# Expert pairs fed by an indirect DMA of stored rows, with the overflow branch behind the output

## The chip, the core and the metric

The kernel runs on one core of a Trainium2 chip. TensorE (PE) multiplies, VectorE (DVE) and ScalarE (ACT) work elementwise, GpSimd (POOL) and SyncE (SP) here mostly issue DMAs. The metric is the device time of one execution in microseconds, the median over the runs of a kernel. Lower is better.

## The reference, cut to what matters

Two transformer layers on 256 tokens of width 1024, all in float32. The second ends in a mixture of 16 experts, which is the part that the change touches:

```python
x = x + gate1 * (merged @ w_out[l])
h2 = rmsnorm(x, norm2_g[l]) * (1.0 + scale2) + shift2
y = hierarchical_moe(h2, ...)         # top-1 group of 4, then top-2 of its 4 experts
x = x + gate2 * y
return rmsnorm(x, final_g)

# in hierarchical_moe
for e in range(N_EXPERTS):            # 16 experts, width 512
    act = jax.nn.silu(hf @ w_gate[e]) * (hf @ w_up[e])
    out = out + combine[:, e:e + 1] * (act @ w_down[e])
```

`combine` is zero for all but two experts of a token, so 256 tokens make 512 uses of an expert.

## The kernel before

The 256 tokens lie in two tiles of 128 rows (`t` = 0, 1) in the slab `X`. All but the experts is matrix work on all tokens; its order was made by a planner with estimated costs (class `Order`). The expert part is written out by hand in `build` (from line 1972) and is not planned: the instructions of an engine stand in the order in which the code calls them.

**The expert pairs.** Two experts at a time are worked on, eight pairs, p = 0 to 7. Each expert takes up to 64 tokens (`CAP`), so a pair fills 128 columns. `routing` gives each token its place `pos` in each expert and its weight `comb`. For each pair:

- `one_hot` (L1493, DVE) compares `pos` with 1 to 64 and makes a 0/1 matrix of tokens by places, and a copy of it multiplied by each token's norm factor `rs`.
- `gather` (L1508) multiplies X by that copy on PE, in sixteen float32 matmuls of 128 columns. The result is the pair's tokens, transposed, in two PSUM banks. ACT empties the first and DVE the second, with the scale and shift of the norm (`ra`).
- `expert_pair` (L1566) runs gate, up and down. One expert works in the left 64 columns of the PE array and one in the right. `w` = 0 is gate, `w` = 1 is up; each has two halves, `q` = 0, 1. Then h = silu(gate) * up on DVE, four transposes of h, ACT's copy `th` of them, and down in two halves of 512 columns.
- `way_back` (L1527) transposes the 0/1 matrix and multiplies it by `comb`; `scatter` (L1547) adds the pair's result to all 256 tokens in four PSUM banks with it.

`mid` is a tuple of functions that `expert_pair` calls on its way: `mid[0]` behind gate (`way_back`), `mid[1]` behind up and ahead of the transposes of h (`gather` of the pair after), `mid[2]` ahead of down (`scatter` of the last half of the pair before), `mid[3]` behind the second half of down.

**Weights.** A pair's weights are twelve chunks of 1 MB, loaded by SP in the order of use, each into a slab from a free list. When the last matmul on a chunk has run, its slab goes back to the list and SP issues the next load into it (`release`, `pump`). Pair 7's last loads, twelve of them, are of 512 KB.

**Overfull experts.** `cnt` is the largest count of an expert. Where it is over 64, `overflow` computes the rest; it is a branch that all engines take or skip, at `mid[3]` of pair 6 (L2007). With these inputs the branch is skipped. The final norm and four output stores follow pair 7.

Of the kernel before, what the change touches and what calls it, by code (L numbers as in the profile page):

```python
# [20 lines left out]
P = 128  # L21
D = 1024
# [24 lines left out]
def constants():  # L47
    i = np.arange(P)
    le = (i[:, None] <= i[None, :]).astype(np.float32)
    lt = (i[:, None] < i[None, :]).astype(np.float32)  # L50
    ge = (i[:, None] >= i[None, :]).astype(np.float32)
    row = i % 64
    head = row % 8
    here = (row < 16) & (head % 2 == i // 64)
    pick = [here & (head // 4 == g) for g in range(2)]
    high = [(row < 8) & (head // 2 % 2 == b) for b in range(2)]
    low = [(row >= 8) & (head // 2 % 2 == b) for b in range(2)]
    fox = np.stack(pick + high + low, axis=1).astype(np.float32)
    fox[:, 2:] *= -1
    cf = np.concatenate(  # L60
        [
            np.eye(P, dtype=np.float32),
            lt,
            np.broadcast_to(np.arange(1, CAP + 1, dtype=np.float32), (P, CAP)),
            np.broadcast_to(np.arange(4, 0, -1, dtype=np.float32), (P, 4)),
            fox,
        ],
        axis=1,
    )
# [251 lines left out]
class Body:  # L321
    def __init__(self, ctx, tc, a, pack):
# [8 lines left out]
        self.big = ctx.enter_context(tc.tile_pool(name="big", bufs=1))  # L331
        self.ps = ctx.enter_context(tc.tile_pool(name="ps", bufs=1, space=bass.MemoryType.PSUM))
# [374 lines left out]
    def setup(self):  # L707
# [4 lines left out]
        self.cf = self.small([P, 2 * P + CAP + 10], "cf")  # L712
# [34 lines left out]
        self.fox = self.cf[:, 2 * P + CAP + 4:]  # L747
# [597 lines left out]
    def res_half(self, t, b, bank):  # L1345
# [13 lines left out]
        if b == 1:  # L1359
            task = self.o.spawn(self.res_scale(t))  # L1360
# [64 lines left out]
    def routing(self):  # L1425
# [60 lines left out]
        self.comb = s("comb", 16)  # L1486
        tt(self.comb.rearrange("p t (g e) -> p t g e", g=4), gb, o1, OP.mult)
# [5 lines left out]
    def one_hot(self, p):  # L1493

        v = self.nc.vector
        buf = self.turn_of("sp").rearrange("p (i t s) -> p i t s", i=2, t=2)
        for t in range(2):
            g, r = buf[:, 0, t], buf[:, 1, t]
            v.tensor_tensor(
                g.rearrange("p (e s) -> p e s", e=2),  # L1500
                self.iota.unsqueeze(1).to_broadcast([P, 2, CAP]),
                self.pos[:, t, 2 * p:2 * p + 2].unsqueeze(2).to_broadcast([P, 2, CAP]),
                OP.is_equal,
            )
            v.tensor_scalar(r, g, self.rs[:, t, 0:1], None, OP.mult)
        return buf

    def gather(self, g):  # L1508

        nc = self.nc  # L1510
        x = self.tmp("ra", 1, D).rearrange("p (k s) -> p k s", k=8)
        for b in range(2):
            ps = self.turn_of("w")
            for j in range(4):
                k = 4 * b + j
                for t in range(2):
                    self.mm(ps[:, j * P:(j + 1) * P], self.x[:, t, k * P:(k + 1) * P], g[:, 1, t], t == 0, t == 1)
            for j in range(4):
                k = 4 * b + j
                out, q = x[:, k], ps[:, j * P:(j + 1) * P]  # L1520
                if b:
                    nc.vector.tensor_scalar(out, q, self.a2[:, k:k + 1], self.modc[:, 3, k:k + 1], OP.mult, OP.add)
                else:
                    self.act(out, q, AF.Identity, scale=self.a2[:, k:k + 1], bias=self.modc[:, 3, k:k + 1])
        return x

    def way_back(self, p, g):  # L1527

        nc = self.nc
        ps = self.turn_of("w")
        for t in range(2):
            self.tr(ps[:, t * P:(t + 1) * P], g[:, 0, t])
        for t in range(2):
            self.mm(ps[:, 256:258], g[:, 0, t], self.comb[:, t, 2 * p:2 * p + 2], t == 0, t == 1)
        gts = []
        for dt in (F32R, F32) if p == 7 else (F32R,):
            gt = self.turn_of("sp")[:, 0:256].bitcast(dt).rearrange("p (t s) -> p t s", t=2)
            self.act(gt, ps[:, 0:256].rearrange("p (t s) -> p t s", t=2), AF.Copy)  # L1540
            gts.append(gt)
        cs = self.tmp("cs", 2, 4)
        for e in range(2):
            nc.vector.tensor_copy(cs[e * 64:(e + 1) * 64, 0:1], ps[e * 64:(e + 1) * 64, 256 + e:257 + e])
        return gts, cs
# [20 lines left out]
    def expert_pair(self, p, x, cs, mid, last=None):  # L1566
# [3 lines left out]
        for w in range(2):  # L1570
            ps = self.turn_of("w")
            for q in range(2):
# [60 lines left out]
    def overflow(self):  # L1633
# [4 lines left out]
        xn = self.sq[0].rearrange("p (t n) -> p t n", t=2)  # L1638
        self.h2 = self.sq[1].rearrange("p (k n) -> p k n", k=8)
        for t in range(2):  # L1640
            self.act(xn[:, t], self.x[:, t], AF.Copy, scale=self.rs[:, t, 0:1])
# [4 lines left out]
        nc.vector.tensor_tensor(co, co, self.comb, OP.mult)  # L1646
# [9 lines left out]
        for e in range(16):  # L1656
# [19 lines left out]
            for t in range(2):  # L1676
                for b in range(2):
# [7 lines left out]
                    y = self.sq[0][:, :512]  # L1685
# [19 lines left out]
    def build(self):  # L1705
# [261 lines left out]
        self.spare(["PP"])  # L1967
# [5 lines left out]
        nxt = self.gather(g)  # L1973
# [4 lines left out]
        for p in range(8):  # L1978
# [10 lines left out]
            def m0(p=p, g=g, prev=prev):  # L1989
# [3 lines left out]
                return self.way_back(p, g)  # L1993

            def m1(ahead=ahead):
                if ahead is not None:
                    box["n"] = self.gather(ahead)
# [16 lines left out]
            prev = self.expert_pair(p, cur, S["pair", p], (m0, m1, m2, m3), self.square if p == 7 else None)  # L2014
# [3 lines left out]
        self.final_norm()  # L2018

    def final_row(self):  # L2020

        self.sums = self.small([P, 2, 3], "sums")
        self.pre = self.small([P, 2], "pre")
        row = self.slab(self.free.pop(), "row_f")
# [23 lines left out]
    def final_norm(self):  # L2048
        nc, v = self.nc, self.nc.vector
        m = self.small([P, 2], "fm")  # L2050
        r = self.small([P, 2], "fr")
        q = self.small([P, 2], "fq")
# [65 lines left out]
```

## Time and profile before

| | us |
|---|---|
| median of 3 runs | 726.47 (726.34 to 728.13) |
| the profiled execution | 727.37 |
| its span in the trace | 725.6 |
| from the first gate matmul of pair 0 to that of pair 7 | 489.0 to 686.7 |

Times in rows are us from the start of the span; a row's second number is how long it lasts. In brackets stands how long the engine idled before, and what ended that. Each float32 matmul has several records in the trace, so that the sixteen matmuls of a gather are 32 records.

### The profile page before, as it was taken

Reading aid. Unit: us, or ns where it says so; the run is one execution under the profiler, and the core shown is the slowest. Engines: PE = TensorE matmul, PEld = TensorE weight load, DVE = VectorE, ACT = ScalarE, POOL = GpSimd, SP = SyncE. Lnnn points to the kernel's source line nnn. Section 1 sums busy time; section 2 is a strip of 40 time slices with the busy share of each in tenths; the row PEclk is TensorE's granted clock in tenths of the full one; section 3 lists DMA queues with packets and bytes.
Section 4 is the critical chain, followed back from the end, with each engine's and each line's share of the span. In section 5 each row is a group of like instructions: output and inputs, shape, how many; then the busy total and the mean of one; then the engine's idle time right before and its main releaser. Section 6 shows DMA issues by size and latency. Waiting matters only on the chain. (4 is left out here: it accounts for less than half of the span.)

```text
span 725.6 us, 10217 instructions
## 1 busy us (share of the span) xinstructions
PE 699.8 (96%) x4028; PEld 506.9 (70%) x4030; DVE 400.4 (55%) x744; ACT 314.6 (43%) x607; POOL 2.2 (0%) x8
## 2 busy tenths in 40 slices
PE   6999999999999988999999999989999999999994
PEld 5999889878878867898877778884344453453432
DVE  6586696896766785768868666452221221212315
ACT  6654465564445586636578545321111110111113
POOL 0000000000000000000000000000000000000000
PEclk9999999999999999999999999989999999999998
DMA  9966666556856661574747957977999999999601
GB/s 359 366 238 229 236 237 231 204 201 217 306 182 228 220 235 63 208 286 163 294 161 280 357 224 293 372 321 322 415 420 423 420 421 421 420 422 416 248 1 58
DMA packets 30373, 201.64 MB, mean 278 GB/s; under 512 B 3825, under 2 KB 4337, under 8 KB 7153
## 3 DMA queue, kind: packets, MB, share of 16 engines
q1 hardware_dynamic: 29968, 200.82, 71.1%
q8 instruction: 33, 0.54, 0.3%
q10 hardware_dynamic: 288, 0.11, 0.1%
q14 instruction: 20, 0.16, 0.1%
q0 software_dynamic: 64, 0.01, 0.0%
HBM read 199.88 MB, written 1.05 MB: 277 GB/s over the span
## 5 line engine op out<-in xcount | busy, mean ns | idle before, releaser
L274 DVE TENSOR_TENSOR w<-ring,w 128x1024 fp32r<-128x1024 f32 (+1 forms) x166 | 156.7, 965 | 80.5 <-ACT w L274 80.1
L274 ACT ACTIVATE w<-ring 128x1024 fp32r<-128x1024 f32 (+1 forms) x166 | 136.3, 849 | 88.8 <-PE d L433 82.0
L433 PE MATMUL d<-w,H 128*128 128x512 f32 x448 | 138.8, 391 | 0.9 <-DVE w L274 0.9
L433 PE MATMUL d<-H,w 128*128 128x256 f32 x672 | 121.8, 283 | 0.0
L433 PEld LDWEIGHTS d<-H,w 128*128 128x128 f32 x672 | 104.6, 192 | 0.1
L433 PE MATMUL d<-w,L 128*128 128x512 f32 x224 | 91.9, 410 | 6.0 <-DVE L L274 6.0
L433 PEld LDWEIGHTS d<-w,H 128*128 128x128 f32 x448 | 84.1, 188 | 18.8 <-DVE w L274 1.6
L433 PE MATMUL d<-L,w 128*128 128x256 f32 x336 | 97.0, 289 | 0.0
L433 PEld LDWEIGHTS d<-L,w 128*128 128x128 f32 x336 | 64.4, 192 | 1.2 <-issue 1.0
L433 PE MATMUL d<-w,YA 128*128 128x512 f32 x224 | 60.6, 394 | 0.0
L433 PEld LDWEIGHTS d<-w,L 128*128 128x128 f32 x224 | 42.1, 188 | 17.0 <-DVE L L274 7.5
L433 PE MATMUL w<-ring,ra 128*64 128x512 f32 x152 | 50.2, 595 | 1.6 <-PEq L2007 1.6
L274 DVE SCALAR_TENSOR_TENSOR acc<-ring,ca,acc 128x1024 f32<-128x1024 f32 x39 | 49.9, 1281 | 1.8 <-DMA ring<-weights 1.6
L433 PEld LDWEIGHTS d<-w,YA 128*128 128x128 f32 x224 | 41.8, 188 | 8.9 <-issue 0.3
L274 ACT ACTIVATE ra<-w,modc,a 128x128 f32<-128x128 f32 x32 | 12.0, 455 | 66.3 <-PE w L433 66.3
L274 ACT ACTIVATE rg<-th 128x512 fp32r<-128x512 f32 x15 | 9.4, 630 | 62.2 <-DVE th L1614 43.6
L274 ACT ACTIVATE th<-w 128x512 f32<-128x512 f32 (+1 forms) x16 | 9.3, 584 | 62.3 <-PE w L433 49.9
L1590 DVE TENSOR_TENSOR th<-th,w 128x512 f32<-128x512 f32 (+1 forms) x9 | 5.6, 628 | 50.2 <-PE w L433 50.2
L433 PEld LDWEIGHTS w<-sp,X 128*128 128x128 f32 x256 | 29.2, 192 | 5.7 <-issue 5.7
L1614 DVE SCALAR_TENSOR_TENSOR th<-w,cs,acc 128x512 f32<-128x512 f32 (+1 forms) x17 | 12.2, 718 | 36.1 <-PE w L433 36.1
L433 PE MATMUL w<-sp,X 128*128 128x128 f32 x256 | 30.7, 278 | 0.0
L433 PEld LDWEIGHTS w<-ring,ra 128*64 128x64 f32 x152 | 15.2, 137 | 21.6 <-issue 21.0
(321 smaller groups left out, 1060.1 us busy)
## 6 DMA issues: line engine op xcount, KB each, us to landing
ring<-weights SPq DMA_DIRECT2D x109, 1024.0 KB, 6.1
spl<-weights SPq DMA_DIRECT2D x16, 1024.0 KB, 11.1
CQ<-weights SPq DMA_DIRECT2D x8, 1024.0 KB, 6.3
AB<-weights SPq DMA_DIRECT2D x6, 1024.0 KB, 10.3
K<-weights SPq DMA_DIRECT2D x5, 1024.0 KB, 7.7
PT<-weights SPq DMA_DIRECT2D x5, 1024.0 KB, 11.9
H<-weights SPq DMA_DIRECT2D x4, 1024.0 KB, 13.6
L<-weights SPq DMA_DIRECT2D x4, 1024.0 KB, 12.1
```

The costliest lines, as they stand in the source:

```text
L274: r = fn(*args, **kw)
L433: self.nc.tensor.matmul(out, lhsT, rhs, start=start, stop=stop)
L1590: nc.vector.tensor_tensor(h[:, c], gate[:, c], res[1][:, c], OP.mult)
L1614: nc.vector.scalar_tensor_tensor(y, out, cw[:, 0:1], self.row_g[1][:, c], OP.mult, OP.mult)
```

## The change

The residual stream x, once complete, is also stored to `xd` in DRAM, by two DMAs that ACT issues (512 KB each). `routing` no longer makes `comb` but `info`: for each token and pair the two weights, the token's number and `rs`. A new function `fetch` multiplies the 0/1 matrix by `info` on PE (four columns), so that each place gets its token's number, weight and norm factor; DVE copies these out of PSUM, the number as an integer. For pairs 1 to 7, POOL then issues an indirect DMA that reads the 128 rows with these numbers from `xd` into `rows_of` (512 KB, two buffers in turn, in the slab `PP`, which the free list no longer gets). `fetched` scales the rows on ACT and transposes them on PE with eight transposes. Pair 0 still uses `gather`. `fetch` for the pair after is called between the two halves of gate (`mid[4]`), `fetched` where `gather` was (`mid[1]`). `one_hot` makes its multiplied copy for pair 0 only. `overflow` follows `final_norm`, and if taken, computes the squares, the final norm and the output anew; it takes its rows from `xd`.

```diff
@@ __init__
+        dram = ctx.enter_context(tc.tile_pool(name="dram", bufs=1, space=bass.MemoryType.DRAM))
+        self.xd = dram.tile([2 * P, D], F32, name="xd")
@@ res_half
         if b == 1:
+            self.nc.scalar.dma_start(self.xd[t * P:(t + 1) * P], self.x[:, t])
             task = self.o.spawn(self.res_scale(t))
@@ routing
-        self.comb = s("comb", 16)
-        tt(self.comb.rearrange("p t (g e) -> p t g e", g=4), gb, o1, OP.mult)
+        self.info = s("info", 8, 4)
+        tt(es, gb, o1, OP.mult)
+        for t in range(2):
+            nc.vector.tensor_copy(self.info[:, t, :, 0:2], es[:, t].rearrange("p g (k e) -> p (g k) e", e=2))
+            nc.vector.tensor_copy(self.info[:, t, :, 2:3], self.token[:, t:t + 1].unsqueeze(1).to_broadcast([P, 8, 1]))
+            nc.vector.tensor_copy(self.info[:, t, :, 3:4], self.rs[:, t, 0:1].unsqueeze(1).to_broadcast([P, 8, 1]))
@@ one_hot
-            v.tensor_scalar(r, g, self.rs[:, t, 0:1], None, OP.mult)
+            if p == 0:
+                v.tensor_scalar(r[:, t], g[:, t].bitcast(F32), self.rs[:, t, 0:1], None, OP.mult)
@@ new
+    def fetch(self, p, g):
+        nc = self.nc
+        ps = self.turn_of("w")
+        for t in range(2):
+            self.mm(ps[:, 0:4], g[1][:, t], self.info[:, t, p], t == 0, t == 1)
...
+        nc.vector.tensor_copy(idx[:, 0:1], ps[:, 2:3])
+        nc.vector.tensor_copy(cs[:, 1:2], ps[:, 3:4])
+        for e in range(2):
+            nc.vector.tensor_copy(cs[e * 64:(e + 1) * 64, 0:1], ps[e * 64:(e + 1) * 64, e:e + 1])
+        if p:
+            rows = self.rows_of[:, (p % 2) * D:(p % 2 + 1) * D]
+            nc.gpsimd.indirect_dma_start(rows, None, self.xd[:, :], bass.IndirectOffsetOnAxis(ap=idx[:, 0:1], axis=0))
+
+    def fetched(self, p):
+        rows = self.rows_of[:, (p % 2) * D:(p % 2 + 1) * D]
+        self.act(rows, rows, AF.Copy, scale=self.cs[p % 2][:, 1:2])
+        x = self.tmp("ra", 1, D).rearrange("p (k s) -> p k s", k=8)
+        for b in range(2):
+            ps = self.turn_of("w")
+            for j in range(4):
+                k = 4 * b + j
+                self.tr(ps[:, j * P:(j + 1) * P], rows[:, k * P:(k + 1) * P])
+            self.shifted(x, b, ps)
+        return x
@@ way_back
-        for t in range(2):
-            self.mm(ps[:, 256:258], g[:, 0, t], self.comb[:, t, 2 * p:2 * p + 2], t == 0, t == 1)
@@ expert_pair
+                if w == q == 0:
+                    mid[4]()
@@ build
-        self.spare(["PP"])
+        self.rows_of = self.slab("PP", "rows_of")
...
+            def m4(p=p, ahead=ahead):
                 if ahead is not None:
-                    box["n"] = self.gather(ahead)
+                    self.fetch(p + 1, ahead)
+
+            def m1(p=p, ahead=ahead):
+                if ahead is not None:
+                    box["n"] = self.fetched(p + 1)
...
                 if p == 6:
                     self.sq = [self.slab(self.free.pop(), "sq") for t in range(2)]
-                    kept = self.pool["w"].pop()
-                    with self.tc.If(rv > CAP):
-                        self.overflow()
-                    self.pool["w"].append(kept)
                     self.final_row()
...
         self.final_norm()
+        with self.tc.If(rv > CAP, preferred_fallthrough_block=False):
+            self.overflow()
+            for c in self.parts(True):
+                self.square(c)
+            self.final_norm()
```

On PE, behind pair 1's up, where the next pair's tokens are made, before (`sp`: the 0/1 matrix times `rs`; `X`: the tokens; `th`: h; `cf`: the identity):

```order
L433 MATMUL w_4669<-YA,ra 64x512
L433 MATMUL w_4697<-sp_4620,X 128x128 x8
L433 MATMUL w_4710<-sp_4620,X 128x128 x8
L449 MATMUL w_4723<-cf,th_4657 128x128 x4
L433 MATMUL d_4475<-rg,sp_4515 128x512 x2
L433 MATMUL d_4477<-rg,sp_4515 128x512 x2
L433 MATMUL w_4733<-PP,th_4694 64x512
```

and now, at the same place:

```order
L436 MATMUL w_4685<-YA,ra 64x512
L452 MATMUL w_4714<-cf,rows_of 128x128 x4
L452 MATMUL w_4723<-cf,rows_of 128x128 x4
L452 MATMUL w_4732<-cf,th_4679 128x128 x4
L436 MATMUL d_4485<-rg,sp_4430 128x512 x2
L436 MATMUL d_4487<-rg,sp_4430 128x512 x2
L436 MATMUL w_4742<-ring_4500,th_4710 64x512
```

Sixteen matmuls have become eight transposes; what stands before and behind them has stayed. The slab `PP` no longer holds weights.

On ACT, from the silu of pair 0's gate to its copy of h's transposes, now (the rows with `ra`, the silu, the copies `sp` and `th` were there before; `cs` holds the norm factors):

```order
L275 ACTIVATE th_4526<-w_4491 128x512
L275 ACTIVATE sp_4430<-w_4537 128x256
L275 ACTIVATE rows_of<-rows_of,cs_4508 128x1024
L275 ACTIVATE ra<-w_4570,modc,a_3585 128x128 x4
L275 ACTIVATE th_4566<-w_4588 128x512
```

The third row is new; it waits for the indirect DMA, and behind it on ACT stand the four that empty the transposes' first bank, and the copy of h that down's matmuls wait for.

On SP, at the end of the program, before (`A`, `spl`: slabs that `overflow` loads weights into; the compare stands far ahead of these rows, behind the weight loads of pair 7):

```order
L1652 DMA spl_6987<-weights 128x2048
L1652 DMA A_7045<-weights 128x2048
L1652 DMA spl_7047<-weights 128x1024 x2
L2007 UNCONDITIONAL_BRANCH x2
L2070 DMA out<-sq 128x512 x4
L2112 UNCONDITIONAL_BRANCH
```

and now:

```order
L467 DMA spl_5393<-weights 128x1024
L467 DMA spl_5395<-weights 128x1024
L2114 DMA out<-sq 128x512 x4
L2059 COMPARE_AND_BRANCH
L2059 UNCONDITIONAL_BRANCH
L1675 DMA xn<-xd 128x1024 x2
```

The compare stands behind the output's stores. When the branch isn't taken, SP goes on to the row behind it, waits there until its DMAs have landed, and jumps over `overflow`'s rows to the end of the program.

## Rows read from the trace of the kernel before

**Rows 1.** The page: busy time of PE; DMA share in 40 slices, in tenths.

```profile
PE 699.8 (96%) x4028; PEld 506.9 (70%) x4030; DVE 400.4 (55%) x744; ACT 314.6 (43%) x607; POOL 2.2 (0%) x8
DMA  9966666556856661574747957977999999999601
```

**Rows 2.** Windows: stretch, length, busy time by engine, PE clock, DMA share, GB/s.

```profile
600.00:620.00 20.00, 20.00 (x111) 9.90 (x112) 3.81 (x11) 3.11 (x7) 0.00 (x0) 1.00 1.01 419
```

**Rows 3.** Timeline of DVE: h = silu(gate) * up of two pairs.

```profile
615.84 0.69 DVE L1590 TENSOR_TENSOR th<-th,w 128x512 f32<-128x512 f32 x1 [6.31 <-PE w L433]
643.87 0.69 DVE L1590 TENSOR_TENSOR th<-th,w 128x512 f32<-128x512 f32 x1 [6.32 <-PE w L433]
```

**Rows 4.** Timeline behind pair 6's up, until down begins.

```profile
671.75 3.84 PE L433 MATMUL w<-sp,X 128*128 128x128 f32 x32
671.89 0.69 DVE L1590 TENSOR_TENSOR th<-th,w 128x512 f32<-128x512 f32 x1 [6.31 <-PE w L433]
...
673.84 1.50 ACT L274 ACTIVATE ra<-w,modc,a 128x128 f32<-128x128 f32 x4 [8.62 <-PE w L433]
...
675.42 0.60 PE L449 MATMUL w<-cf,th 128*128 128x128 f32 x4
...
676.06 0.60 ACT L274 ACTIVATE th<-w 128x512 f32<-128x512 f32 x1 [0.72 <-PE w L449]
...
676.88 0.64 PE L433 MATMUL w<-spl,th 128*64 128x512 f32 x1
```

**Rows 5.** Timeline of PE: pair 0, first matmul of gate's second half; then DVE.

```profile
492.51 0.59 PE L433 MATMUL w<-CQ,ra 128*64 128x512 f32 x1
...
491.84 0.19 DVE L1487 TENSOR_TENSOR rt_comb<-rt_goh,rt_o 128x32 f32<-128x32 f32 x1
...
493.06 0.29 DVE L1505 TENSOR_SCALAR sp<-sp,rs 128x128 f32<-128x128 f32 x1
```

**Rows 6.** Timeline of PE in pair 6: gate's halves begin; `way_back`'s product.

```profile
657.00 0.64 PE L433 MATMUL w<-YC,ra 128*64 128x512 f32 x1
...
660.49 0.59 PE L433 MATMUL w<-spl,ra 128*64 128x512 f32 x1
...
664.30 0.51 PE L433 MATMUL w<-rt_comb,sp 128*128 128x2 f32 x4
```

**Rows 7.** Timeline of DVE and PE behind the branch of pair 6.

```profile
685.35 1.66 DVE L2027 TENSOR_SCALAR row_f<-cf,cols 128x128 f32<-128x128 f32 x8 [2.54 <-DVEq L2007]
...
686.67 3.65 PE L433 MATMUL w<-ring,ra 128*64 128x512 f32 x16 [1.57 <-PEq L2007]
```

**Rows 8.** Timeline of SP: the last load before the pairs, the next ones.

```profile
477.68 0.33 SPq L464 DMA_DIRECT2D PP<-weights  x1
492.70 0.80 SPq L464 DMA_DIRECT2D ring<-weights  x2
```

**Rows 9.** Tile ring at 643.8: a load of pair 7's gate, second half.

```profile
L464 SPq DMA_DIRECT2D ring<-weights x1: 328/328/328, 643.8 to 643.8; - x1
...
DMA to landing us min/median/max: 19.6/19.6/19.6
```

**Rows 10.** Timeline of PE: the first matmul that uses it.

```profile
690.17 0.59 PE L433 MATMUL w<-ring,ra 128*64 128x512 f32 x1
```

**Rows 11.** Tile acc: a load of 4 KB that POOL issued.

```profile
L1256 POOL DMA_DIRECT2D acc<-ada_b x1: 756/756/756, 408.8 to 408.8; - x1
...
DMA to landing us min/median/max: 5.8/5.8/5.8
```

**Rows 12.** Tile ring at 408.3: a weight load that SP issued.

```profile
L464 SPq DMA_DIRECT2D ring<-weights x1: 328/328/328, 408.3 to 408.3; - x1
...
DMA to landing us min/median/max: 10.5/10.5/10.5
```

**Rows 13.** The page: ACT on tiles of 1024 columns; landing of the stores.

```profile
L274 ACT ACTIVATE w<-ring 128x1024 fp32r<-128x1024 f32 (+1 forms) x166 | 136.3, 849 | 88.8 <-PE d L433 82.0
...
out<-sq SPq DMA_DIRECT2D x4, 256.0 KB, 2.4
```

More of the change, by code (lines that the diff above doesn't have):

```diff
@@ L66, in constants @@
             fox,
+            np.stack([i, i + P], axis=1).astype(np.float32),
         ],
@@ L711, in setup @@
             self.load(self.x[:, t], a["x"][t * P:(t + 1) * P])
-        self.cf = self.small([P, 2 * P + CAP + 10], "cf")
+        self.cf = self.small([P, 2 * P + CAP + 12], "cf")
         nc.scalar.dma_start(self.cf[:, 0:P], a["cf"][:, 0:P])
@@ L746, in setup @@
         self.rev = self.cf[:, 2 * P + CAP:2 * P + CAP + 4]
-        self.fox = self.cf[:, 2 * P + CAP + 4:]
+        self.fox = self.cf[:, 2 * P + CAP + 4:2 * P + CAP + 10]
+        self.token = self.cf[:, 2 * P + CAP + 10:]
         self.le = k[:, 1792:1920]
@@ L1495, in one_hot @@
         v = self.nc.vector
[L1496 removed]
+        buf = self.turn_of("sp").bitcast(F32R)
+        g = buf[:, 0:256].rearrange("p (t s) -> p t s", t=2)
+        r = self.rows_of[:, 0:256].rearrange("p (t s) -> p t s", t=2)
         for t in range(2):
[L1498 removed]
             v.tensor_tensor(
[L1500 removed]
+                g[:, t].rearrange("p (e s) -> p e s", e=2),
                 self.iota.unsqueeze(1).to_broadcast([P, 2, CAP]),
@@ L1504, in one_hot, with gather @@
             )
-            v.tensor_scalar(r, g, self.rs[:, t, 0:1], None, OP.mult)
-        return buf
-    def gather(self, g):
-        nc = self.nc
+            if p == 0:
+                v.tensor_scalar(r[:, t], g[:, t].bitcast(F32), self.rs[:, t, 0:1], None, OP.mult)
+        return buf, g.bitcast(F32), r
+    def gather(self, r):
         x = self.tmp("ra", 1, D).rearrange("p (k s) -> p k s", k=8)
@@ L1516, in gather, with shifted @@
                 for t in range(2):
[L1517 to L1524, printed above, removed]
-        return x
-    def way_back(self, p, g):
+                    self.mm(ps[:, j * P:(j + 1) * P], self.x[:, t, k * P:(k + 1) * P], r[:, t], t == 0, t == 1)
+            self.shifted(x, b, ps)
+        return x
+    def shifted(self, x, b, ps):
+        for j in range(4):
+            k = 4 * b + j
+            out, q = x[:, k], ps[:, j * P:(j + 1) * P]
+            if b:
+                self.nc.vector.tensor_scalar(out, q, self.a2[:, k:k + 1], self.modc[:, 3, k:k + 1], OP.mult, OP.add)
+            else:
+                self.act(out, q, AF.Identity, scale=self.a2[:, k:k + 1], bias=self.modc[:, 3, k:k + 1])
+    def fetch(self, p, g):
         nc = self.nc
@@ L1533, in way_back @@
         for t in range(2):
-            self.tr(ps[:, t * P:(t + 1) * P], g[:, 0, t])
-        for t in range(2):
-            self.mm(ps[:, 256:258], g[:, 0, t], self.comb[:, t, 2 * p:2 * p + 2], t == 0, t == 1)
[L1537 to L1545, printed above, removed]
+            self.mm(ps[:, 0:4], g[1][:, t], self.info[:, t, p], t == 0, t == 1)
+        idx = self.small([P, 2], f"idx{p % 2}", mybir.dt.uint32) if p < 3 else self.idx[p % 2]
+        cs = self.small([P, 4], f"cs{p % 2}") if p < 3 else self.cs[p % 2]
+        self.idx[p % 2], self.cs[p % 2] = idx, cs
+        nc.vector.tensor_copy(idx[:, 0:1], ps[:, 2:3])
[11 more added lines that the diff above has]
+            ps = self.turn_of("w")
+            for j in range(4):
+                k = 4 * b + j
+                self.tr(ps[:, j * P:(j + 1) * P], rows[:, k * P:(k + 1) * P])
+            self.shifted(x, b, ps)
+        return x
+    def way_back(self, p, g):
+        ps = self.turn_of("w")
+        for t in range(2):
+            self.tr(ps[:, t * P:(t + 1) * P], g[1][:, t])
+        gt = g[0][:, 256:].rearrange("p (t s) -> p t s", t=2)
+        self.act(gt, ps[:, 0:256].rearrange("p (t s) -> p t s", t=2), AF.Copy)
+        return [gt, gt.bitcast(F32)]
     def scatter(self, p, m):
@@ L1637, in overflow @@
         assert len(tags) >= 4
-        xn = self.sq[0].rearrange("p (t n) -> p t n", t=2)
-        self.h2 = self.sq[1].rearrange("p (k n) -> p k n", k=8)
+        xn = self.slab(tags.pop(), "xn").rearrange("p (t n) -> p t n", t=2)
+        self.h2 = self.slab(tags.pop(), "h2").rearrange("p (k n) -> p k n", k=8)
         for t in range(2):
-            self.act(xn[:, t], self.x[:, t], AF.Copy, scale=self.rs[:, t, 0:1])
+            nc.sync.dma_start(xn[:, t], self.xd[t * P:(t + 1) * P])
+            self.act(xn[:, t], xn[:, t], AF.Copy, scale=self.rs[:, t, 0:1])
             o.spawn(self.h2_block(t, xn))
@@ L1645, in overflow @@
         nc.vector.tensor_scalar(co, self.pos, CAP + 0.5, None, OP.is_gt)
-        nc.vector.tensor_tensor(co, co, self.comb, OP.mult)
+        for t in range(2):
+            c2 = co[:, t].rearrange("p (k e) -> p k e", e=2)
+            nc.vector.tensor_tensor(c2, c2, self.info[:, t, :, 0:2], OP.mult)
         def load(i, name, e, k0, c):
@@ L1972, in build @@
         g = self.one_hot(0)
-        nxt = self.gather(g)
+        nxt = self.gather(g[2])
         next(steps, None)
@@ L1992, in m0 @@
                     add_last(p, prev)
-                return self.way_back(p, g)
-            def m1(ahead=ahead):
+                if p == 0:
+                    self.fetch(0, g)
+                return self.way_back(p, g), self.cs[p % 2]
+            def m4(p=p, ahead=ahead):
                 if ahead is not None:
-                    box["n"] = self.gather(ahead)
+                    self.fetch(p + 1, ahead)
+            def m1(p=p, ahead=ahead):
+                if ahead is not None:
+                    box["n"] = self.fetched(p + 1)
             def m2(p=p, prev=prev):
@@ L2013, in build @@
                 rv = nc.values_load(self.cnt[0:1, 0:1])
-            prev = self.expert_pair(p, cur, S["pair", p], (m0, m1, m2, m3), self.square if p == 7 else None)
+            prev = self.expert_pair(p, cur, S["pair", p], (m0, m1, m2, m3, m4), self.square if p == 7 else None)
             nxt, g = box.get("n"), ahead
@@ L2023, in final_row @@
         self.pre = self.small([P, 2], "pre")
+        self.last = [self.small([P, 2], n) for n in ("fm", "fr", "fq")]
         row = self.slab(self.free.pop(), "row_f")
@@ L2049, in final_norm @@
         nc, v = self.nc, self.nc.vector
-        m = self.small([P, 2], "fm")
-        r = self.small([P, 2], "fr")
-        q = self.small([P, 2], "fq")
+        m, r, q = self.last
         for t in range(2):
```

3 lines of the change are left out of this document (2 added, 1 removed).

## The prediction

> **What bounds the kernel now.** I read the page first. PE is busy for 96% of the span, and the DMA digits are at 9 through the last third [rows 1], which is the eight expert pairs. There both are full: in 20 us PE works for 20.00, at its full clock, and the DMA share is 1.01 at 419 GB/s [rows 2]. Two full resources need a second look at which one the end follows. The same instruction of two neighbouring pairs lies 28.03 us apart [rows 3]. A pair's weights are 12 chunks of 1.049 MB, 12.6 MB, which at 419 GB/s take 30.0 us. So the stream is the slower of the two by 2 us a pair, and PE is never late only because the loads started far ahead: a load of pair 7's gate lands at 643.8 + 19.6 = 663.4 [rows 9], and its first matmul runs at 690.17 [rows 10], 26.8 us later. PE sets the end; the stream's lead is what any gain on PE is paid from.
>
> Next, the place that the change replaces. In the timeline behind a pair's up, PE is never idle: the gather's 32 records take from 671.75 to 675.6, h's transposes follow, and down begins at 676.88, behind ACT's copy of h [rows 4]. So what is saved there moves the next pair, until another engine in that place is late.
>
> **The change part by part, in us.**
>
> *Gather to transposes, seven times.* The sixteen matmuls take 3.84. Eight float32 transposes from SBUF are like the four of h, 0.60 for four with the pipe's end [rows 4]; eight end at 1.1 to 1.2. By PE alone 2.7 is saved a pair. But ACT becomes late: it empties the first four transposes (1.50), and only then copies h (0.60) [rows 4]. From the end of up: four transposes 0.65, ACT 1.50, ACT 0.60, and 0.24 from the copy's end to down's matmul, as now (676.06 + 0.60 to 676.88, 0.22): 3.0. Now it is 676.88 - 671.75 = 5.13. Saved: 2.1 a pair, 14.7 in seven. h itself is ready (671.89 + 0.69 = 672.58) before the eight transposes end, so DVE isn't late. The ends are 7 x 2.7 = 18.9, where ACT's copy hides in some way, and 7 x 1.5 = 10.5, where transposes are at the pace of 0.3 each; I take 14.7, for which every piece has its row.
>
> *The product with `info`* replaces that with `comb` (0.51, [rows 6]), with the same four records; it stands between gate's halves and not beside two transposes. Net 0, between -0.1 and +0.2 a pair.
>
> *Pair 0's wait.* There the product comes at 492.51 [rows 5], and needs `info` and the next 0/1 matrix. DVE has its `comb` at 492.03 and both matrices of `one_hot` at 493.35 [rows 5]. Six small copies come in (0.15 to 0.2 each, issued closer than that: 0.9) and two multiplications of 0.29 go out. PE waits until about 493.6: +1.1, once.
>
> *The rows' way.* In pair 6 gate begins at 657.00, its second half at 660.49, up ends at 671.75 [rows 4, 6]. The row numbers are there 3.5 + 0.5 + 0.2 = 4.2 after gate's start. PE wants the scaled rows 14.8 after it, and ACT needs 0.85 to 1.0 for 1024 columns [rows 13]; so POOL's DMA has 9.5 from issue to landing. No row shows an indirect DMA. The nearest is POOL's load of 4 KB, 5.8 to landing [rows 11]. With 512 KB the transfer adds 1.25 if it has the DMA engines alone (0.524 MB at 419 GB/s), and 3.7 if its rows of 4 KB take turns with weight rows of 8 KB: 7.0 to 9.5. I take 8.3. That POOL's load landed 5.8 after its issue, while a weight load issued 0.5 before it took 10.5 [rows 11, 12], says that it doesn't stand in line behind the weights. The Trainium skill, "DMA: Bandwidth & Descriptors", section on queues, rings and completion order, states the same: each engine goes round between the queues that have work. What it doesn't say is how long POOL takes to make descriptors out of row numbers.
>
> *The stream.* Seven gathers of 1.25 come on top of the weights: 8.7. The slab PP holds rows now, so its load at 477.68 falls away, and each later chunk comes one place later behind the restart at 492.70 [rows 8]: 2.5. The weights' landing is delayed by 11.2 by pair 7. The store of x (1 MB, 2.5) lies before 492.70, in a stretch where no slab is free and the queue runs empty; its two issues on ACT fall into ACT's waits. Both at 0; without that cover the store costs the stream its 2.5.
>
> *The branch.* Gone at pair 6: PE's 1.57 [rows 7], -1.6. DVE's 2.54 lies beside PE's work. At the end, PE, ACT, DVE and POOL jump while the output is under way (2.4 to landing, [rows 13]): nothing. But SP jumps only after the last landing, and nothing runs beside it. A skipped branch has cost PE 1.57 and DVE 2.54 [rows 7], SP's is unseen; I take 2.0, and 0.2 for waiting on more semaphores: +2.2, between 0.2 and 3. The Trainium skill, "Runtime: NRT & Kernel Launch", section on instruction fetch mechanics, says that a taken branch stalls only when its target lies outside the two pages of instructions at hand; SP's jump over a hundred loads could stay inside. By that the sum would be 2.0 lower.
>
> *Sum.* -14.7 + 1.1 - 1.6 + 2.2 = -13.0. Made against the profiled execution, 727.4 (its span of 725.6 and 1.8 around it): 714.4. The median before is 0.9 below that execution, so 713.5 on that basis; I forecast 714.
>
> *Does the stream hold?* At the load of rows 9 PE comes 14.7 - 1.1 + 1.6 = 15.2 earlier and the weights 11.2 later: 26.4 of 26.8 is used. It just holds. It also caps the gain: had PE saved 2.7 a pair, it would wait for weights from pair 6 on, and the end would move by no more than 26.8 - 11.2 = 15.6 less the tail, to 714.0. Both limits give nearly the same time, which is why I trust it from below more than from above.
>
> **The rivals.**
>
> *The stream decides.* A gather costs it more than its bytes: read in 4 KB pieces through another queue, say twice 1.25. Then the weights are 20 late, PE can be 6.8 earlier, and the time is 727.4 - 6.8 + 2.2 = 722.8. For it: the share is 1.01, so every byte counts. Against: 4 KB rows are what the 512 KB weight loads have as well, and the share stays full there. The Trainium skill's DMA page, section on issuing engines not being separate queues, speaks for it too, in that POOL's DMA can't escape the sixteen engines; that much is in my 8.7 already.
>
> *The rows come late* (this ends on the other side). In each of pairs 0 to 6 ACT waits for the landing, and PE behind it, with h's transposes and down behind that on the same queue. Each us past the 9.5 costs 7. From 1.9 late (11.4 from issue to landing) the gain of 13 is gone, and at 12.5 it is 727.4 - 13 + 21 = 735. If the rows stood behind the weights like SP's own load (19.6, [rows 9]) it would be 714.4 + 7 x 10.1 = 785. For it: my estimate has only 1.2 to spare, and the weights' queue gets deeper as PE gets faster. Against: rows 11 and 12.
>
> *Nothing is saved in the pairs*, because the place behind up is held by ACT for as long as the gather held it: then the wait of pair 0 and the tail remain, 727.4 + 1.1 - 1.6 + 2.2 = 729. Rows 4 speak against it, since each piece is shorter.
>
> **How the numbers follow.** My forecast 0.52. The stream 0.18, anywhere between 715 and 723. Rows late 0.27, of which 0.11 by under 1.5 (715 to 723), 0.06 by so much that nothing is left, 0.10 by more. Nothing saved 0.03. A measurement of this kernel tells 0.3% (2.2 us) from no change. Faster: 0.52 + 0.18 + 0.11 = 0.81; the same 0.06 + 0.01 = 0.07; slower 0.12. The range goes from 709 (SP's jump free, and weights delayed by 8 and not 11, with the transposes' 2.7) to 723 (the stream at twice the price, or rows 1.3 late).
>
> **What would show it.** In the changed profile h's instructions of neighbouring pairs lie 25.9 apart; right behind up PE runs eight transposes of about 1.2 in all, and ACT's copy of h ends 2.7 after up. POOL's DMAs land 7 to 9.5 after issue. In pair 7 PE has next to no lead over the weights. Behind the last store's landing SP shows a gap of about 2. Wrong would be: ACT's scaling of rows that ends idle time with a DMA as releaser (rows late), PE waits for weight loads from pair 3 or 4 on (the stream), a period near 28 without waits (nothing saved).

## The result

The changed kernel takes 717.7 us (median of 4 runs, 715.5 to 718.6) against 727.3 beside it: a ratio of 0.985, interval 0.983 to 0.987, a gain of 1.5%. The forecast was 714.0, in a range of 709 to 723. Six later runs of the same kernel gave a median of 716.4. It is faster by the mechanism that was forecast, and by some 3 us less.

### The profile page after: what moved, and what is told of

It is laid out like the page before. It is cut to its first block, busy times and chain, and to the rows that moved or that the text cites. A ratio compares the mean times of both kernels' runs of the same rounds, so it can differ in the third digit from the quotient of the medians.

```text
span 716.8 us, 9935 instructions
## 1 busy us (share of the span) xinstructions
PE 684.7 (96%) x3862; PEld 487.3 (68%) x3862; DVE 397.6 (55%) x752; ACT 321.1 (45%) x613; POOL 9.1 (1%) x15
## 4 chain that ended last, share of the span: by engine, by line
PE 80%; DMA 8%; DVE 5%; ACT 4%; issue 1%; POOLq 0%; ACTq 0%; DVEq 0%
PE d L436 52%; PE w L436 24%; DMA rows_of<-xd,idx 8%; PE w L452 3%; DVE w L275 2%; ACT ra L275 1%; ACT rows_of L275 1%; DMA X<-x 1%; ACT th L275 1%; DVE L L275 1%; ACT xs L275 0%; DVE PP L275 0%; DVE X L275 0%; ACT sq L275 0%; DVE sw L275 0%
## 5 line engine op out<-in xcount | busy, mean ns | idle before, releaser
L436 PE MATMUL w<-ring,ra 128*64 128x512 f32 x128 | 47.2, 598 | 0.0
L436 PE MATMUL w<-spl,ra 128*64 128x512 f32 x96 | 32.7, 597 | 0.0
L436 PEld LDWEIGHTS w<-ring,ra 128*64 128x64 f32 x128 | 13.4, 136 | 19.8 <-issue 19.5
L436 PE MATMUL w<-ring,th 128*64 128x512 f32 x72 | 25.1, 597 | 1.2 <-ACT th L275 1.1
L275 ACT ACTIVATE rows_of<-rows_of,cs 128x1024 f32<-128x1024 f32 x7 | 8.0, 1148 | 38.7 <-DMA rows_of<-xd,idx 38.7
```

The source lines that it names most:

```text
L275: r = fn(*args, **kw)
L436: self.nc.tensor.matmul(out, lhsT, rhs, start=start, stop=stop)
```

## The profile after

The profiled execution took 718.64, with a span of 716.8. The page, in the order of [rows 1], with the chain's second row (shares of the span along the chain that ended last):

```profile
PE 684.7 (96%) x3862; PEld 487.3 (68%) x3862; DVE 397.6 (55%) x752; ACT 321.1 (45%) x613; POOL 9.1 (1%) x15
...
DMA  9966657456857552664765876995999999999971
...
PE d L436 52%; PE w L436 24%; DMA rows_of<-xd,idx 8%; PE w L452 3%; DVE w L275 2%; ACT ra L275 1%; ACT rows_of L275 1%; DMA X<-x 1%; ACT th L275 1%; DVE L L275 1%; ACT xs L275 0%; DVE PP L275 0%; DVE X L275 0%; ACT sq L275 0%; DVE sw L275 0
```

PE's busy time has gone down by 15.1. The chain now runs through the indirect DMA. Its 8% are the DMA's whole flights in six of the seven pairs (8.8 to 9.6 each), during which PE had other work, and not time that PE lost. What PE did wait is in the view of waits, for PE alone, from 480 on (us in total, times, longest):

```profile
PE w L436 <- ACT th L275: 2.9, 7, 1.3
PE w L452 <- ACT rows_of L275: 1.8, 4, 0.5
PE w L452 <- DVE th L1624: 0.7, 1, 0.7
PE d L436 <- DVE rg L1658: 0.6, 1, 0.6
PE w L436 <- DVE sp L1509: 0.5, 1, 0.5
```

The second row is the rows' being late. There is no row with a weight load as releaser: the stream holds. Where it stands is seen at chunk `L` of pair 7's gate, issued at 653.95:

```profile
L467 SPq DMA_DIRECT2D L<-weights x1: 327/327/327, 654.0 to 654.0; - x1
...
DMA to landing us min/median/max: 21.1/21.1/21.1
```

It lands at 675.04, and the timeline has PE's first matmul on it at 678.22. Of a lead of 26.8 [rows 9, 10] 3.2 are left.

Behind pair 6's up, the place of [rows 4], the timeline of PE and ACT:

```profile
662.64 1.15 ACT L275 ACTIVATE rows_of<-rows_of,cs 128x1024 f32<-128x1024 f32 x1 [5.53 <-DMA rows_of<-xd,idx]
...
663.84 1.09 PE L452 MATMUL w<-cf,rows_of 128*128 128x128 f32 x8 [0.29 <-ACT rows_of L275]
664.54 1.51 ACT L275 ACTIVATE ra<-w,modc,a 128x128 f32<-128x128 f32 x4 [0.75 <-PE w L452]
...
664.77 0.60 PE L452 MATMUL w<-cf,th 128*128 128x128 f32 x4
...
665.92 0.61 ACT L275 ACTIVATE th<-w 128x512 f32<-128x512 f32 x1
...
666.59 1.50 PE L436 MATMUL w<-ring,th 128*64 128x512 f32 x5 [0.29 <-ACT th L275]
```

Up ends at 663.55; the scaled rows are there at 663.79, 0.24 later. In pairs 1 to 3 they are just in time, in pairs 4 and 5 they come 0.5 late, and h of neighbouring pairs, DVE's row as in [rows 3], lies 26.58 apart there (28.03 before):

```profile
637.09 0.69 DVE L1624 TENSOR_TENSOR th<-th,w 128x512 f32<-128x512 f32 x1 [10.62 <-PE w L436]
...
663.67 0.69 DVE L1624 TENSOR_TENSOR th<-th,w 128x512 f32<-128x512 f32 x1 [10.60 <-PE w L436]
```

At the end of the program the view of DMAs, 40 slices of 707 to 717 (GB/s in each, then the queues):

```profile
GB/s 0 0 0 0 0 0 0 115 344 385 336 360 426 361 336 361 369 360 189 57 66 74 66 25 57 25 25 25 0 0 0 0 0 0 0 33 0 0 0 0
DMA packets 581, 1.10 MB, mean 110 GB/s; under 512 B 64, under 2 KB 64, under 8 KB 576
...
q14 instruction: 4, 0.03, 1.2%
q8 instruction: 1, 0.02, 0.6%
```

The stores run at 340 to 430 GB/s for 2.5 us, and then trickle for another 2.5 at 25 to 75: at 420 for sixteen DMA engines that is one to three of them that are behind. Just ahead of the trickle packets of instructions ran between the stores' (16 KB, 0.93 us from 710.1; then two of 8 KB, 0.44 and 0.41, from 710.4 and 711.0), and some packets of the stores took up to 0.50 there and not 0.08. The stores land 4.5 to 5.0 after their issue, where it was 2.4 in the median [rows 13]:

```profile
DMA to landing us min/median/max: 4.5/4.8/5.0
```

The span comes apart into three stretches that can be compared between all the kernels below: up to pair 0's first gate matmul, from there to the end of the last matmul, and the tail. Before: 489.0, 227.7 and 8.9. After: 489.3, 215.1 and 12.4. So the pairs gave 12.6, and the tail took 3.5 back. (The first stretch, which no edit touches but for the store of x and the row numbers, ends between 487.6 and 490.5 in the executions below. PE's granted clock from 480 to 489 was 0.80 to 0.89 in the seven where it ended at 489.0 or later, and 0.94 to 0.98 in the five where it ended earlier: part of that time is at 1.2 GHz and the rest at 2.4. So a difference of 1 or 2 us between two executions means little, and the stretches tell more.)

## The experiments

**1. No branch.** The changed kernel without the branch and its body.

```diff
         self.final_norm()
-        with self.tc.If(rv > CAP, preferred_fallthrough_block=False):
-            self.overflow()
-            ...
```

> The changed kernel without the branch and its body (the overflow case is left out; these inputs don't take it). Theory (the tail): in the changed kernel the first store takes 4.5 us to land and not 2.0, because fetches of instructions for the jumps (16 KB and two of 8 KB) run beside the stores, and SP jumps after the last landing; without the branch the last store lands about 2.6 after its issue, the span ends 1.1 after that, and the time is 3.5 us below the changed kernel's, about 714. Rival (the stores are slow for another reason, such as a store to DRAM after the pairs' stream): the landing stays near 5 us and only SP's jump of about 1 us goes, 716.7.

713.2 (712.7 to 714.4), as the theory has it: the stores land in 2.0 to 2.7 again. Pairs 214.4, tail 8.9: the tail is that of the kernel before, and what the branch costs at the end is 3.5.

**2. The branch back at pair 6**, all else as changed.

```diff
                 if p == 6:
                     self.sq = ...
+                    kept = self.pool["w"].pop()
+                    with self.tc.If(rv > CAP):
+                        self.overflow()
+                    self.pool["w"].append(kept)
                     self.final_row()
...
-        with self.tc.If(rv > CAP, preferred_fallthrough_block=False):
-            ...
```

> The changed kernel with the branch back behind pair 6's down, as in the kernel before. Theory: the tail's 3.5 us go, PE's stall of 1.6 at the branch comes back, so about 1.9 us below the changed kernel, 715.8. Rival (the place of the branch costs the same at either end): no difference beyond 0.5 us.

732.9 (732.6 to 733.3), slower than the kernel before. All theories missed. Timelines of DVE and PE behind the branch:

```profile
695.74 1.66 DVE L2071 TENSOR_SCALAR row_f<-cf,cols 128x128 f32<-128x128 f32 x8 [25.57 <-SPq L2050]
...
696.76 3.75 PE L436 MATMUL w<-row_f,ones 128*128 128x512 f32 x4 [10.21 <-DVE row_f L2071]
```

Line 2050 is the branch. `final_row` behind it takes a slab, and must wait for SP to be through the branch. SP comes to it only when it has issued all loads that stand ahead of it (its compare is at 685.32), and leaves it when these have landed (695.03). In the kernel before, SP's compare was at 673.96 and its last landing at 683.70, 1.4 ahead of PE's arrival at the branch: the place was cheap because the stream led by 26.8. The change spends that lead, and with it the place. PE's clock goes too (stretch, length, busy times, PE clock, DMA share, GB/s):

```profile
640.00:676.00 36.00, 31.94 (x150) 11.97 (x146) 7.23 (x17) 5.90 (x11) 0.94 (x1) 0.99 1.01 419
676.00:686.60 10.60, 9.98 (x32) 3.14 (x32) 0.00 (x0) 0.00 (x0) 0.00 (x0) 0.70 1.02 408
```

PE stood still from 672.46 to 676.56, at its own jump (more on this in experiment 8); the 32 matmuls of pair 7's gate behind it took 9.98 at a granted 0.70 (at 1.2 GHz from 675.6 to 682.4, then at 2.4), and take 7.09 at full clock.

**3. Only the branch moved**, in the kernel before.

```diff
                 if p == 6:
                     ...
-                    kept = self.pool["w"].pop()
-                    with self.tc.If(rv > CAP):
-                        self.overflow()
-                    self.pool["w"].append(kept)
                     self.final_row()
...
         self.final_norm()
+        with self.tc.If(rv > CAP, preferred_fallthrough_block=False):
+            self.overflow()
+            ...
```

> The kernel before with the branch alone moved behind the output's stores; gathers stay on PE. Theory: +3.5 at the tail and -1.6 at pair 6, about 1.9 us slower than before. Rival (the branch in pair 6 costs its 1.6 and the tail nothing): 1.6 faster. My prediction on record had +2.2 and -1.6, 0.6 slower.

727.9 (12 runs), a ratio of 1.000, 0.999 to 1.001. By stretches the pairs take 226.0 (1.7 less: the jump of [rows 7]) and the tail 12.3 (3.4 more). That is 1.7 on balance, near the theory's 1.9, and the medians show none of it; profiles and medians differ here by as much as first stretches do, and which is nearer stays open. It is no gain, in any case.

**4. The rows asked for half a gate earlier.** The product and the indirect DMA stand ahead of gate for pairs 2 to 7; the 0/1 matrix is made a pair earlier.

```diff
-            ahead = self.one_hot(p + 1) if p < 7 else None
+            ahead = self.one_hot(1) if p == 0 else later
...
+                if p < 6:
+                    box["a"] = self.one_hot(p + 2)
@@ expert_pair
+            if w == 0 and p:
+                mid[4]()
-                if w == q == 0:
+                if w == q == 0 and not p:
                     mid[4]()
```

> The changed kernel with the product for the row numbers and the indirect DMA at the start of gate and not between its halves, for pairs 2 to 7 (the 0/1 matrices are made one pair earlier for this); 3.5 us more for the rows to land. Theory (rows late by 0.1 to 0.5 a pair): PE no longer waits for ACT's scaled rows, the distance of neighbouring pairs falls from 26.3 to about 25.9, and the time by 2 us, 715.7. Rival (PE's period is set by ACT's copy of h or by the stream, and the rows' landing doesn't matter): the distance stays 26.3 and the time 717.7.

714.4 (713.5 to 714.9); ratio 0.981, 0.979 to 0.982. Pairs 212.0, tail 11.7. No PE wait for rows is left in the view, and a new one begins, for the weights (view of waits, PE, from 480 on):

```profile
PE w L436 <- ACT th L275: 2.5, 7, 1.3
PE w L452 <- DVE th L1626: 0.7, 1, 0.7
PE d L436 <- DVE rg L1660: 0.6, 1, 0.6
PE w L436 <- DVE sp L1509: 0.5, 1, 0.5
PE w L436 <- DMA L<-weights: 0.2, 1, 0.2
```

The last row is small, but pair 7's gate, whose two experts wait for different chunks, takes 8.4 from its first to its last matmul, and 7.1 in the changed kernel. The transposes now follow up without a gap (up ends at 659.60), and h of two pairs (634.11 and 659.72) lies 25.6 apart, less than the expected 25.9 (experiment 6 has the reason):

```profile
659.54 1.09 PE L452 MATMUL w<-cf,rows_of 128*128 128x128 f32 x8
660.47 0.65 PE L452 MATMUL w<-cf,th 128*128 128x128 f32 x4
...
662.28 0.65 PE L436 MATMUL w<-ring,th 128*64 128x512 f32 x2 [0.24 <-ACT th L275]
```

This is the fastest version that keeps the whole computation, and beats both kernels.

**5. Both together:** the early fetch and no branch.

> The fetch half a gate earlier, and no branch at all (the code for overfull experts is left out). Theory (the two losses, rows late in the pairs and the branch's 3.5 in the tail, stand beside each other and add): 714.4 of the early fetch, less 3.5 to 4.5, is 710.4, with pair distances of 25.6 and a tail of 8.9 from the last matmul to the end. Rival (the weights have become the limit once the pairs are at 25.6, so that what the tail gives back is lost to waits for weight loads in pairs 6 and 7): 712 or more, with PE waits named after weight loads.

712.1 (711.0 to 712.9). Pairs 212.4, tail 8.9. The tail is that of the kernel before; the pairs gain nothing over experiment 4. Pair 7's gate takes 8.8 from its first to its last matmul, not 7.1, and PE waits inside it:

```profile
675.36 0.64 PE L436 MATMUL w<-L,ra 128*64 128x512 f32 x1 [0.66 <-DMA L<-weights]
```

The lead is used up at the place where 3.2 of it was left. Both expectations hold in part: the losses do stand apart, and the stream is the next limit, worth 1.7, of which 1.3 was there in experiment 4.

**6. Half the rows' bytes**, without the branch: only the left 512 columns are stored and fetched, the right half of the tokens is zeros.

```diff
-            nc.gpsimd.indirect_dma_start(rows, None, ...)
+            nc.gpsimd.indirect_dma_start(rows[:, 0:512], None, ...)
```

> No branch, and the indirect DMA brings only the left 512 of the 1024 columns (2 KB a row; the right half of the tokens is zeros from one memset, and the store of x is halved too; scaling and transposes as before). Compared with the changed kernel without a branch (713.2). Theory (the landing is about 4.2 to the first packet plus a transfer that takes turns with the weights' packets): landing 9.1 falls to about 7, the waits on ACT's scaled rows (1.4 in the trace) go, pair distance 25.7: 711.3. Rival (what POOL and the queue need for 128 rows sets the landing, bytes hardly count): landing stays at 8.5 to 9, time 713.

712.5 (712.2 to 712.8); pairs 212.7, no PE wait for rows. The indirect DMAs of pairs 2 to 7 (engine, operation, count: duration in ns, first and last start), first in the changed kernel, then here:

```profile
L1555 POOL DMA_INDIRECT rows_of<-xd,idx x6: 939/940/982, 521.6 to 653.5; - x6
...
DMA to landing us min/median/max: 8.8/9.1/9.3
```

```profile
L1555 POOL DMA_INDIRECT rows_of<-xd,idx x6: 944/944/996, 520.6 to 651.0; - x6
...
DMA to landing us min/median/max: 6.9/7.4/7.8
```

256 KB less lands 1.7 sooner. So 512 KB cost about 3.4 beside the weights, and 5.7 of the 9.1 are there whatever the bytes, if the half of them is a fair measure of the other. Expected was a landing of 7 and a time of 711.3: the landing is nearly right, the time 1.2 too low, since the pairs' distance is 26.0 (h at 635.15 and 661.12), not 25.7. Around pair 6, where up ends at 661.00:

```profile
645.84 0.64 PE L436 MATMUL w<-ring,ra 128*64 128x512 f32 x1
...
660.93 1.09 PE L452 MATMUL w<-cf,rows_of 128*128 128x128 f32 x8
...
663.67 0.65 PE L436 MATMUL w<-ring,th 128*64 128x512 f32 x2 [0.22 <-ACT th L275]
```

The rows are in time here and in experiment 4, and still the pairs are 0.34 further apart here. What differs is where the product with `info` stands. Between gate's halves, as here, it is 15.16 from gate's first matmul to up's end; in experiment 4 it is 14.47, and 0.43 for the product ahead of it (14.82 in the kernel before). So experiment 4 does not measure the rows alone: of its 3.1 in the pairs the rows are about 2.4, the product's place about 2.0 in six pairs, and pair 7's longer gate takes 1.3 back.

**7. A short body at the end.** The branch stays, but skips only the final norm.

```diff
         with self.tc.If(rv > CAP, preferred_fallthrough_block=False):
-            self.overflow()
-            for c in self.parts(True):
-                self.square(c)
             self.final_norm()
```

> The changed kernel with the branch in its place, but with a body of only the final norm and its stores (the computation for overfull experts is left out). Theory (the tail's 3.5 come from jumping over a long body, by fetches of instructions amid the stores and at SP's jump): stores land 2.0 to 2.7 after issue, tail of 9 to 9.5, time 713.5 to 714.3, as the kernel without a branch (713.2) and a little more. Rival (the branch itself costs it, by compare, jump and the waits for semaphores at its edges): 716.5 to 717.7, with a landing of 4.5 to 5 after issue.

714.1 (713.0 to 715.4). Pairs 215.3, as in the changed kernel; tail 8.9. The view of DMAs, 707 to 717, as above:

```profile
GB/s 0 0 0 0 0 0 0 0 41 344 393 361 385 385 377 385 393 385 393 336 17 0 0 0 0 0 0 0 0 0 0 0 0 0 0 0 0 0 0 0
DMA packets 576, 1.05 MB, mean 105 GB/s; under 512 B 64, under 2 KB 64, under 8 KB 576
...
q1 hardware_dynamic: 576, 1.05, 27.6%
```

No packet of instructions, no trickle, stores landing in 2.5, none of their packets over 0.11. So the 2.3 by which the stores land late go with the length of what is skipped: behind the long body engines have to get their instructions from further on, on the DMA engines that the stores need. The other 1.3 of the 3.5 is SP's, and this run doesn't separate it. SP's semaphore waits at the branch, in the changed kernel, then here (count, duration in ns, first and last start):

```profile
L2059 SPq EVENT_SEMAPHORE  x8: 17/17/17, 710.4 to 714.7; - x8
L2059 SPq EVENT_SEMAPHORE  x4: 17/17/17, 710.4 to 710.6; - x4
```

With the long body SP waits there until the stores have landed, and only then jumps and goes through its last waits; with the short one it waits for none of them and passes the branch in 0.6 (compare at 710.25, first wait behind it from 710.85), while the stores are under way. The length of the body and the waits at its edge have changed together. The Trainium skill, "Runtime: NRT & Kernel Launch", section on instruction fetch mechanics, has the rule that a taken branch stalls for a fetch when its target isn't in the two pages at hand; the runs with the long and the short body agree with it on four engines (from the branch to the next instruction PE takes 3.9, DVE 4.0, ACT 0.4 and SP 0.5 with the long body, and 0.2 each with the short one), while POOL, which jumps at 653.4, takes 0.16 with both.

**8. Two other places for the branch**, on top of experiment 4: behind pair 7's last down, and ahead of it.

```diff
             prev = self.expert_pair(p, ...)
...
+        kept = self.pool["th"].pop()
+        with self.tc.If(rv > CAP, preferred_fallthrough_block=False):
+            self.overflow()
+            for c in self.parts(True)[:2]:
+                self.square(c)
+        self.pool["th"].append(kept)
         self.gathered(prev[1], self.scatter(7, prev))
         self.square(prev[1])
         self.final_norm()
```

> The fetch half a gate earlier, and the branch ahead of pair 7's last scatter instead of behind the output's stores; all weights have landed there. Theory (the branch is dear at pair 6 because SP gets to it only when the last loads are issued, and dear at the end because instructions are fetched amid the stores; where neither holds it costs what DVE's gap was in the kernel before): stores land 2.0 to 2.7 after issue again, tail of 8.9 from the last landing on as without a branch, plus 1.6 to 2.5 on PE and DVE: 712 to 713. Rival (the branch costs the same anywhere, by fetching code for five engines): 714.4 or more; and over 716 if engines wait there for SP.

715.4 (714.9 to 716.6). Stores land in 2.4 again, but PE stands still:

```profile
702.92 2.05 PE L436 MATMUL w<-th,sp 128*128 128x256 f32 x4 [3.65 <-issue]
```

The rival was right: behind the last down the jump costs 3.3 over experiment 5, no less than the 2.4 at the end.

```diff
             def m2(p=p, prev=prev, box=box):
...
+                if p == 7:
+                    kept = self.pool["th"].pop()
+                    with self.tc.If(rv > CAP, preferred_fallthrough_block=False):
+                        self.overflow()
+                    self.pool["th"].append(kept)
```

> The fetch half a gate earlier, and the branch ahead of pair 7's down, where SP has no load left to issue and DVE and ACT have no work that PE waits for. Theory (the branch is a jump of 1.6 on PE where the other engines' jumps and SP's loads are out of the way, and it was dear at pair 6 only since SP came to it late): the kernel without a branch (712.1) and 1.6 to 2, 713.7 to 714.1; a little less if PE would have waited for down's weights anyhow; tail of 8.9. Rival (the branch costs 3.3 as behind the last down, wherever engines jump over the long body): 715.4. Rival of pair 6 (PE waits for SP's loads to land): 718 or more.

720.2 (718.0 to 720.8). The time is that of the rival of pair 6, but the run does not show the rival's reason:

```profile
695.92 1.08 PE L436 MATMUL w<-ring,th 128*64 128x512 f32 x1 [5.47 <-SPq L2053]
```

SP has issued its last load at 685.45 and passed its compare at 685.83; that load lands at 695.53, and the timeline names SP. But PE's own branch instruction, on its sequencer, runs from 690.64 to 695.65, so PE could not have gone on before that, whatever SP did. PE's branch here, then behind the last down (ns min/median/max, first and last start):

```profile
L2053 PEldq COMPARE_BRANCH  x2: 95/2550/5006, 690.1 to 690.6; - x2
L2062 PEldq COMPARE_BRANCH  x2: 95/1696/3296, 696.3 to 699.5; - x2
```

In every run with the long body a packet of 16 KB of instructions starts during the longer of these, and PE goes on 1.3 to 1.5 after that packet's end. With the stream over, behind the last down, the packet starts 0.9 after the branch, and the branch takes 3.3. Here, with loads still under way, it starts 2.5 after it (5.0 in all); in experiment 2, beside the full stream, 3.4 after it (5.9 in all). So loads under way lengthen the jump itself. Whether PE would also have waited for SP's last landing this run can't tell, since the two end 0.12 apart. The wait for SP is shown in experiment 2, on DVE, which had its jump behind it at 675.04 and still stood until 695.74.

**9. The changed kernel again**, beside them.

> The changed kernel as it is, for its time beside the versions that differ from it by one part: 717.7, between 716.5 and 718.7, that is 3.3 above the one with the early fetch (714.4) and 3.5 to 4.5 above the one without a branch (713.2). Rival (the median of four runs was off, and the parts are worth less): under 716.5.

716.4 (715.3 to 719.7, 6 runs), on the rival's side by 0.1. Pairs 215.3, tail 12.0. Against this median the early fetch is worth 2.0, the branch 3.2, a short body 2.3; against the first one 1.3 more each. By stretches it is 3.1 in the pairs, 3.5 in the tail and 3.5 in the tail.

## Why the prediction was right, and where not

*Gather to transposes.* The mechanism is right and so is its size, where the rows are in time: without their waits (experiment 6) the pairs take 212.7, and the forecast's terms give 227.7 - 14.7 + 1.1 - 1.6 = 212.5. Pairs are 26.0 apart there, 25.9 were forecast. ACT's copy of h is what down waits for, as said, for 0.22 to 0.29. That the sum is met so closely is partly luck, for two terms are off and cancel. The place behind up gives 2.39 a pair and not 2.1: from the transposes to down it is 2.74 in experiment 6, not 3.0, since ACT's copy of h begins before its work ahead has ended, and down follows the copy by 0.06 (in the text 0.24, which is 0.22 by its own row). And the product with `info`, forecast at 0 (-0.1 to +0.2), costs 0.34 a pair between gate's halves.

*The rows' way.* This is the step that failed, and it costs 2.4 (215.1 against 212.7; 1.7 against experiment 1's 214.4, where the rows were a little less late). The budget was 9.5 from issue to landing, with 1.2 to spare. In pair 6 the row numbers' DMA is issued 5.1 after gate's start (653.53 - 648.39), not 4.2, since POOL's DMA begins 0.7 after the numbers are copied (at 652.78, and so in the pairs before), for which the sum had nothing; landing takes 9.0 there and 9.1 in the median, not 8.3 (the range of 7.0 to 9.5 held, but for the first DMA's 9.6); ACT's scaling 1.15, not 0.85 to 1.0. Up ends 15.2 after gate's start, not 14.8, which gives 0.4 back. 1.2 - 0.9 - 0.7 - 0.2 + 0.4 is -0.2: the rows are 0.2 late, as the timeline has it. The rival "the rows come late" was right in its first part (by under 1.5), with 0.11 for it.

*Pair 0.* Forecast +1.1, and a saving of 2.1 behind up: 1.0 gained. The gain is 0.2 (27.64 to pair 1, 27.85 before). The wait for `info` was 0.5, not 1.1. But pair 0 makes two products with `info`, its own and pair 1's, where there was one with `comb`: 0.6 that the sum left out. Its rows come 0.5 late, and ACT, which empties the transposes before it copies h, holds down back by 1.3 (0.7 before).

*The stream.* 26.4 of 26.8 was to be used, with PE 15.2 earlier. PE came 11.9 earlier at pair 7's gate and 3.2 are left, so the weights came 11.7 later: forecast 11.2. The cap, too, was right: the end was to move by 15.6 at most before the tail, and in experiments 4 and 5 it moves by 15.6 and 15.3 (227.7 to 212.0 and 212.4) and stops at the weights.

*The branch.* -1.6 at pair 6 is -1.7 (experiment 3). That was its price beside the longer pairs only: left there beside the shorter ones it makes the kernel 15 slower than the changed one, and 20 slower than without a branch (experiments 1 and 2). The tail was forecast at +2.2 and is +3.5. Of this 1.3 is SP, from the last landing to the end (2.4 against 1.1), less than the 2.2 forecast; 2.3 is the last store's landing (5.0 against 2.7), which the text had at "nothing", since the other engines jump while the output is under way. They do, and with the long body their jumps delay the output (experiment 7).

*Sum.* Pairs -12.6, not -15.2; tail +3.5, not +2.2; first stretch +0.3: -8.8 in the profiled executions, not -13.0. Both errors point the same way, and the forecast of 714 lay outside what the kernel's first four runs show, though well inside its range.

## What to carry over

A transfer that replaces work is worth what was forecast only if it is asked for early enough: with a slack worked out from three estimates, each of them a little off, put the request as early as its inputs allow, which here gave 2 to 3 us together with a better place for the product. A branch costs what stands around it: behind it an engine can have to wait for SP's loads to land, and while loads are under way the jump itself takes longer, so a place is cheap only as long as the stream leads; and a skipped long body behind the output brings instruction fetches into the stores' way. Before a lead is spent, look for what else lives on it. A wait's named releaser is a lead and no proof: see whether the waiting engine was free before.

## What was not expected of the hardware

- An indirect DMA of 128 rows of 4 KB occupies POOL for 0.94 us, and lands 8.8 to 9.3 after its issue beside a full stream of weights (the first one 9.6); with rows of 2 KB 6.9 to 7.8.
- One packet of 16 KB and two of 8 KB of instructions (0.9, 0.4 and 0.4 us) amid 1 MB of stores go with a last landing 2.3 later (5.0 after issue against 2.7), more than they take; why it is so much more is not shown.
- PE's jump over the long body takes 3.3 to 3.7 with no loads under way, 5.0 and 5.9 beside loads. In the kernel before it took 3.4, and PE's queued matmuls hid all but 1.6 of it.
- Idle time of PE is followed by a lower clock: after it stood still from 690.45 to 695.92 in the last run of experiment 8, the 32 matmuls of down took 8.1 us at a granted 0.66 (1.2 GHz until 701.45, then 2.4), and 5.4 at full clock in the kernel before:

```profile
695.90:704.10 8.20, 8.11 (x32) 3.31 (x32) 1.01 (x2) 0.90 (x2) 0.00 (x0) 0.66 0.02 6
```

- Between executions of these kernels the end of the stretch ahead of the pairs varies by up to 2.9 us (487.6 to 490.5) with PE's clock there, which is as much as the parts of this change are worth.
